# YOCO hybrid trunk on one core: deferred activations held in source order, an early GpSimd select, and two late evictions

## The chip, the cores and the metric

One core of one Trainium2 chip runs the kernel. The metric is device time in microseconds (us) of one execution, the median of several runs. The engines are TensorE (PE: matmuls), VectorE (DVE), ScalarE (ACT), GpSimd (POOL) and SyncE (SP, which issues most DMAs). Each engine works through its own queue in order; they wait for each other through semaphores.

## The reference, cut to what matters

Two layers on x of 1024 x 1024 float32. Layer one is a chunked gMLP, layer two attention in a sliding window of 128:

```
u, v, z = split(rms_norm(x) @ w_in, 3)      # each 1024 x 2048
u = gelu(u);  v = layer_norm(gelu(v))
s = einsum(causal(w_s), v per chunk of 128, 8 groups of 256 channels) + b_s
h = x + rms_norm((u * s * silu(z)) @ w_out)
k, v = rms_norm(h) @ w_k, @ w_v
q, z = split(rms_norm(h) @ w_in_b, 2)
o = softmax with sinks over a band of 128 (ALiBi), 16 query heads, 4 kv heads
out = h + rms_norm((o * silu(z)) @ w_out_b)
```

All matmuls are to be exact to nearly float32.

## The kernel before

**Matmuls.** Every operand is split into a high and a low part (`split`, L104: ScalarE copies the high part, L105; VectorE subtracts for the low part, L106; with a gain it is L109 and L110). A product is then three matmuls into one PSUM bank (`mm3`, L168: lines L169, L170, L171), each 128x512.

**Stage v** (`v_layer`, to about 145 us). v = x @ w_v is made in seven Strassen-Winograd products, in the order m = 1, 2, 5, 6, 7, 4, 3, for two halves Q = 0 and 1 of the columns, each m in two steps u = 0, 1. There are two sets of four PSUM banks, `vb` (m = 1, 6, 7, 4 accumulate in it) and `vc` (m = 2, 5, 3). At the ends of m = 1, 6 and 7 ScalarE copies the four tiles of `vb` out (L209); PE can add the next product to a bank of `vb` only after its copy. VectorE adds `vc` to the slots (L206). A finished block gets its gelu from `done` (L390 to L392): one ScalarE instruction per tile, `vslot<-vslot,rx` with the row scale `rx`, and one VectorE `bn_stats`. For two blocks of Q = 0 these are put off to a later step (`late`); for Q = 1 the first block's are called right at the end of m = 2. `rx` is 1/rms of x's rows: a small VectorE instruction (L178) and a power on GpSimd (L179). `broadcast_rstd` makes diagonals `dg` from it (ScalarE L279, VectorE L280) and spreads them with four matmuls (L284).

The inputs of each step come ahead of it: `prep(n + 2)` loads the next weight piece (SP), adds or subtracts pieces on VectorE (L206, `sch`, `vraw`) and splits them.

**Stage uz** (`uz_layer`, 150 to 480 us). 16 quads: for each of 8 groups g one of u and one of z, again seven products; `ub` is a PSUM bank that products 1, 6, 7 and 4 of a quad share, and ScalarE copies it out between them (L209). `normalise(g)` scales the eight pieces of the loaded v (VectorE L614), `spatial` makes the gating matmuls (L621), `finish` takes the silu of z (L630) and the u quads get four gelus (L697). Gelu and silu lie in different activation tables: ScalarE loads a table (ACT_TABLE_LOAD) at each change between them. The causal mask is a GpSimd affine_select on `wc` (L593), one per group.

**Stages out, q, kv, z.** `qz_four` (L958) makes four 128-column tiles of q or z. Its `evac` for q (L973 to L981) makes two ScalarE and two VectorE instructions per tile. `kv_phase` follows with the next weights, which `wnext` takes and splits one ahead.

**What sets the order.** The engines' orders are not those of the source. The framework's scheduler places each traced instruction on its engine's queue; an instruction that was traced later can stand ahead of one that waits for something late. `tc.keep_in_program_order(ins)` holds an instruction behind the one that was traced before it on its engine; it adds no wait.

Of the kernel before, what the change touches and what calls it, by code (L numbers as in the profile page):

```python
# [7 lines left out]
F32 = mybir.dt.float32  # L8
# [3 lines left out]
AF = mybir.ActivationFunctionType  # L12
ALU = mybir.AluOpType
# [9 lines left out]
G = 8  # L23
# [27 lines left out]
def tile_yoco(  # L51
# [111 lines left out]
    def wnext():  # L163
        w = weights.get()
        weights.ahead()
        return w
# [36 lines left out]
    HT = KT // 2  # L203

    def add(out, a, b, op, eng=None):
        (eng or nc.vector).tensor_tensor(out, a, b, op)  # L206

    def copy(out, a):
        nc.scalar.activation(out, a, AF.Copy)  # L209

    def xrow(h, t):
        return x[h * TH + t * P:h * TH + (t + 1) * P, :]
# [85 lines left out]
    def v_layer(ahead):  # L298
# [88 lines left out]
            dst = vd[2 * Q + i][4 * j:4 * j + 4]  # L387
            nc.scalar.dma_start(out=dst.rearrange("n p c -> p n c"), in_=block)

        def done(out, src, i, j, t, Q):  # L390
            nc.scalar.activation(out, src, AF.Gelu_apprx_tanh, scale=rx[j][:, t:t + 1])
            nc.vector.bn_stats(stats[:, 4 * j + t, 2 * Q + i], out)  # L392

        ORDER = (1, 2, 5, 6, 7, 4, 3)
# [24 lines left out]
        for k in range(2):  # L419
# [4 lines left out]
                                           ALU.mult, ALU.subtract)  # L424
            nc.vector.tensor_tensor(p0[1][:, cs], r0[:, cs], p0[0][:, cs].bitcast(F32), ALU.subtract)
        ready[0] = p0
        r1_ = load(raws.take("v1"), wv_in[0, 1])
        for k in range(2, 4):
            split_scaled(T[1][0][:, k], T[1][1][:, k], xa[:, 0, k], g(0, k))
# [10 lines left out]
        for n, (Q, m, u) in enumerate(steps):  # L440
# [24 lines left out]
            elif n >= 4:  # L465
                step(side)

            late = {(7, 0): (a1, 0), (3, 0): (e67, 1)}.get((m, u)) if Q == 0 else None
            if late:
                for t in range(4):  # L470
                    done(late[0][t], late[0][t], late[1], late[1], t, Q)
                store(slots[late[1]], late[1], late[1], Q)
            if u == 0:
                continue
            for t in range(4):
                if m == 1:
                    a1.append(slots[0][:, t])
                    copy(a1[t], ps[t])
                elif m == 2:
                    add(a1[t], a1[t], ps[t], ALU.add)  # L480
                    if Q:
                        done(a1[t], a1[t], 0, 0, t, Q)
                elif m == 6:
                    if t == 0:
                        e6 = big.tile([P, 4, TH], F32, tag="P1_3", name=f"ve6_{Q}")
                    copy(e6[:, t], ps[t])
                elif m == 7:
                    e67.append(slots[1][:, t])
                    copy(e67[t], ps[t])
                    add(e67[t], e67[t], bank_c[t], ALU.add)  # L490
                    if Q:
                        done(e67[t], e67[t], 1, 1, t, Q)
                elif m == 4:
                    c = slots[Q][:, t]
                    done(c, ps[t], 1, 0, t, Q)
                elif m == 3:
                    add(e6[:, t], e6[:, t], ps[t], ALU.add)
                    done(e6[:, t], e6[:, t], 0, 1, t, Q)
            block = {3: (e6, 0, 1), 4: (slots[Q], 1, 0)}.get(m)
            if Q and m in (2, 7):  # L500
                block = (slots[0], 0, 0) if m == 2 else (slots[1], 1, 1)
            if block:
                store(*block, Q)
            if m == 3:
# [10 lines left out]
    def uz_layer():  # L515
# [95 lines left out]
        def normalise(g):  # L611
            vg = grp[g]["vg"]
            for n in range(NB):
                nc.vector.tensor_scalar(vg[:, n], vg[:, n], mv[:, n, 0:1], ve[:, n:n + 1], ALU.subtract, ALU.mult)  # L614

        def spatial(g, i, j):
            d = grp[g]
# [9 lines left out]

        def finish(g, i, j):
            z = grp[g][1][i, j]
            nc.scalar.activation(z, z, AF.Silu)  # L630
            add(z, z, grp[g][0][i, j], ALU.mult)
            m = {(0, 0): 1, (1, 0): 2, (1, 1): 3}.get((i, j))
            if m:
                nc.sync.dma_start(out=td[m][g], in_=z)
# [30 lines left out]
        for q in range(len(quads) + 1):  # L665
# [20 lines left out]
            if q > 0:  # L686
                product(q - 1, 3, pcc, False)
                add(pc[0, 1], pc[0, 1], pcc, ALU.add)
                scale(pc[0, 1], 1)
                if pz:  # L690
                    finish(pg, 0, 1)
                    sums(pg)
                    del grp[pg]
                else:
                    for i in range(2):
                        for j in range(2):
                            nc.scalar.activation(pc[i, j], pc[i, j], AF.Gelu_apprx_tanh)  # L697
                del ops[q - 1]
            if not live:
                break  # L700
# [254 lines left out]
    half = [slice(0, 64), slice(64, P)]  # L955
    vt = big.tile([P, NB, 256], F32, tag="P1_1", name="vt")

    def qz_four(h, which, m, n, evac):  # L958

        tag = "s" if (h, which, m) in ((0, 0, 4), (0, 1, 0)) else "mm"  # L960
        ps = [bank(tag, f"qz{h}_{which}_{m + i}") for i in range(4)]
        for kq in range(4):
            hi, lo = (t.rearrange("p (m k c) -> p m k c", m=4, k=2) for t in wnext())
            for i in range(4):
                for kk in range(2):
                    k = 2 * kq + kk
                    mm3(ps[i], hi[:, i, kk], lo[:, i, kk], n[0][:, k], n[1][:, k], k == 0, k == KT - 1)
                if kq == 3:
                    evac(m + i, ps[i])
                yield  # L970

    def q_phase(h, n, q):
# [24 lines left out]
    def kv_phase(h, n):  # L997
        pk = [bank("mm", f"pk{h}_{i}") for i in range(2)]
        pv = [bank("mm", f"pv{h}_{i}") for i in range(2)]
        for kp in range(4):  # L1000
            hi, lo = wnext()
            for kk in range(2):
                k = 2 * kp + kk
                o = kk * 512
# [297 lines left out]
```

## Time and profile before

| | us |
|---|---|
| median of 3 runs | 1050.8 (1050.23 to 1050.91) |
| the profiled execution | 1051.19 |
| its span, first to last instruction | 1049.4 |
| PE busy in it | 1038.2 (99%) |
| DVE, ACT, POOL busy | 731.8, 579.8, 199.5 |
| granted TensorE clock, share of full speed | 0.998 |

The page is read in this order: the busy share of each engine, PE's list of waits, and then PE's timeline at each wait with the timelines of the engines named there. The span is shorter than the execution's own time by 1.8 us, which lies outside the first and last instruction.

### The profile page before, as it was taken

The numbers are of one execution on the slowest core, as the hardware profiler recorded it, in microseconds if no ns is written. First come the engines' busy times: TensorE is split into PE (matmuls) and PEld (weight loads), VectorE is DVE, ScalarE is ACT, GpSimd is POOL, SyncE is SP. The second block draws the span as 40 slices with busy tenths as digits, with TensorE's granted clock in tenths as the row PEclk, the third lists the DMA queues.
The fourth block names the chain that finished last, engine by engine and source line by source line (L and its number), as shares of the span: only waits on it lengthen the run. The fifth ranks groups of instructions, "written<-read, shape, count | busy, mean of one in ns | idle before, by whom it ended". The sixth has DMA issues, their size and how long they took to land.

```text
span 1049.4 us, 13678 instructions
## 1 busy us (share of the span) xinstructions
PE 1038.2 (99%) x4994; PEld 854.8 (81%) x4994; DVE 731.8 (70%) x1244; ACT 579.8 (55%) x998; POOL 199.5 (19%) x153
## 2 busy tenths in 40 slices
PE   9999999999999999999999999999999999999997
PEld 7878888888888888888888888888888777877776
DVE  6987566867768668677696587765247786667763
ACT  6584344565565465655444465654466665786631
POOL 0500003253442552530200000100001111011120
PEclk9999999999999999999999999999999999999999
DMA  8878242324333333247998543532322121211363
GB/s 309 271 262 292 101 171 94 116 101 146 126 117 120 123 134 116 101 140 265 320 354 282 195 167 93 200 102 82 99 81 66 56 81 61 81 61 62 121 220 121
DMA packets 80899, 157.56 MB, mean 150 GB/s; under 512 B 5824, under 2 KB 32704, under 8 KB 80832
## 3 DMA queue, kind: packets, MB, share of 16 engines
q1 hardware_dynamic: 76320, 148.01, 41.4%
q10 hardware_dynamic: 4512, 8.68, 2.3%
q8 instruction: 39, 0.64, 0.3%
q14 instruction: 28, 0.23, 0.1%
HBM read 125.21 MB, written 31.46 MB: 149 GB/s over the span
## 4 chain that ended last, share of the span: by engine, by line
PE 93%; DVE 3%; DMA 2%; ACT 1%; issue 0%; SPq 0%; DVEq 0%; POOLq 0%; ACTq 0%
PE qz L169 6%; PE ob L169 6%; PE ub L169 6%; PE qz L171 6%; PE ub L170 6%; PE ub L171 6%; PE ob L171 6%; PE ob L170 6%; PE qz L170 6%; PE s L1058 3%; PE uc L170 3%; PE uc L169 3%; PE uc L171 3%; PE sp L621 3%; PE oc L169 2%; PE oc L171 2%
## 5 line engine op out<-in xcount | busy, mean ns | idle before, releaser
L110 DVE SCALAR_TENSOR_TENSOR wlo<-raw_w,gn,whi 128x512 fp32r<-128x512 f32 x80 | 58.5, 757 | 62.2 <-ACT whi L109 62.0
L169 PE MATMUL qz<-n_hi,whi 128*128 128x512 f32 x256 | 100.9, 394 | 0.0
L171 PE MATMUL qz<-n_hi,wlo 128*128 128x512 f32 x256 | 99.8, 390 | 1.1 <-DVE wlo L110 1.1
L170 PE MATMUL qz<-n_lo,whi 128*128 128x512 f32 x256 | 99.9, 390 | 0.0
L109 ACT ACTIVATE whi<-raw_w,gn 128x512 fp32r<-128x512 f32 x80 | 54.8, 716 | 56.8 <-PE qz L170 36.6
L1073 ACT ACTIVATE pr<-pr,mx 128x129 f32<-128x129 f32 x128 | 50.1, 393 | 39.8 <-DVE mx L1069 39.8
L169 PEld LDWEIGHTS qz<-n_hi,whi 128*128 128x128 f32 x256 | 48.1, 188 | 15.8 <-issue 5.7
L105 ACT ACTIVATE uzhilo_g<-f 128x1024 fp32r<-128x1024 f32 x31 | 32.9, 1060 | 49.2 <-PE uc L171 43.3
L171 PEld LDWEIGHTS qz<-n_hi,wlo 128*128 128x128 f32 x256 | 48.0, 188 | 11.8 <-DVE wlo L110 1.5
L170 PEld LDWEIGHTS qz<-n_lo,whi 128*128 128x128 f32 x256 | 48.1, 188 | 9.3
L106 DVE TENSOR_TENSOR uzhilo_g<-f,uzhilo_g 128x1024 fp32r<-128x1024 f32 x31 | 38.6, 1245 | 19.9 <-ACT uzhilo_g L105 19.9
L209 ACT ACTIVATE uz_slots<-ub 128x512 f32<-128x512 f32 x48 | 28.3, 590 | 42.4 <-PE ub L171 39.2
L169 PE MATMUL ub<-T,whi_g 128*128 128x512 f32 x128 | 50.7, 396 | 0.0
L169 PE MATMUL ub<-T,uzhilo_g 128*128 128x512 f32 x128 | 50.5, 395 | 0.0
L171 PE MATMUL ub<-T,wlo_g 128*128 128x512 f32 x128 | 49.9, 390 | 0.0
L171 PE MATMUL ub<-T,uzhilo_g 128*128 128x512 f32 x128 | 49.9, 390 | 0.0
L170 PE MATMUL ub<-T,uzhilo_g 128*128 128x512 f32 x128 | 49.9, 390 | 0.0
L170 PE MATMUL ub<-T,whi_g 128*128 128x512 f32 x128 | 49.8, 389 | 0.0
L169 PE MATMUL uc<-T,uzhilo_g 128*128 128x512 f32 x124 | 48.9, 395 | 0.0
L170 PE MATMUL uc<-T,uzhilo_g 128*128 128x512 f32 x124 | 48.3, 389 | 0.0
L171 PE MATMUL uc<-T,uzhilo_g 128*128 128x512 f32 x124 | 48.3, 389 | 0.0
L105 ACT ACTIVATE whi_g<-raw_uz 128x1024 fp32r<-128x1024 f32 (+1 forms) x31 | 26.5, 854 | 36.8 <-PE ua L170 14.3
(334 smaller groups left out, 3078.3 us busy)
## 6 DMA issues: line engine op xcount, KB each, us to landing
raw_uz<-in_wuz_in_dram SPq DMA_DIRECT2D x32, 512.0 KB, 3.4
raw_w<-in_wqz_dram SPq DMA_DIRECT2D x32, 512.0 KB, 3.5
td<-uz_slots SPq DMA_DIRECT2D x56, 256.0 KB, 2.2
orawP2a<-td SPq DMA_DIRECT2D x28, 512.0 KB, 4.1
raw<-in_wv_in_dram SPq DMA_DIRECT2D x17, 512.0 KB, 4.8
vg<-vd SPq DMA_DIRECT2D x8, 1024.0 KB, 5.3
orawP2b<-in_wo_a_dram SPq DMA_DIRECT2D x16, 512.0 KB, 8.2
vraw<-in_wv_in_dram SPq DMA_DIRECT2D x13, 512.0 KB, 4.8
```

Source lines behind the costliest of these rows:

```text
L105: nc.scalar.activation(hi, src, AF.Copy)
L106: nc.vector.tensor_tensor(lo, src, hi.bitcast(F32), ALU.subtract)
L109: nc.scalar.activation(hi, src, AF.Copy, scale=g)
L110: nc.vector.scalar_tensor_tensor(lo, src, g, hi.bitcast(F32), ALU.mult, ALU.subtract)
L169: nc.tensor.matmul(out, lhsT=a_hi, rhs=b_hi, start=start, stop=False, skip_group_check=True)
L170: nc.tensor.matmul(out, lhsT=a_hi, rhs=b_lo, start=False, stop=False, skip_group_check=True)
L171: nc.tensor.matmul(out, lhsT=a_lo, rhs=b_hi, start=False, stop=stop, skip_group_check=True)
L209: nc.scalar.activation(out, a, AF.Copy)
L621: nc.tensor.matmul(psv[:, n], lhsT=d["vg"][:, 4 * j + n, i * P:(i + 1) * P], rhs=d["wc"], start=True, stop=True)
L1058: nc.tensor.matmul(pss[par][:, g, w0:256], lhsT=q[par][:, m, bs_], rhs=w[par][:, p, ks], start=g + k == 0, stop=g + k == 2, skip_group_che ...
L1073: nc.scalar.activation(pr[:, i], pr[:, i], AF.Exp, bias=mx[:, i:i + 1], scale=-1.0, accum_out=dn[:, i:i + 1])
```

## The change

Four edits.

1. In `v_layer`, the put-off gelus (`late`) are held in source order on ScalarE, and for Q = 1 the gelus of the first block move from the end of m = 2 to the step (5, 0), which makes them put-off ones too.
2. In `uz_layer`, the scalings of `normalise`, the silus of `finish` and the gelus of u are held in source order, silus and gelus except for the last group.
3. In `v_layer`, behind GpSimd's first two casts, GpSimd copies 128x2 numbers into `mv[:, 0]` (a tile that is written for good at the end of the stage) and runs a 128x2 affine_select on it.
4. In `qz_four`, for the second four tiles of the first q phase (h = 0, m = 4), the evictions of tiles 2 and 3 (qz_0_6, qz_0_7) are put off into `kv_phase`, behind its first `wnext()`.

```diff
+    pin = tc.keep_in_program_order
...
-        def done(out, src, i, j, t, Q):
-            nc.scalar.activation(out, src, AF.Gelu_apprx_tanh, scale=rx[j][:, t:t + 1])
+        def done(out, src, i, j, t, Q, put_off=False):
+            gelu = nc.scalar.activation(out, src, AF.Gelu_apprx_tanh, scale=rx[j][:, t:t + 1])
+            if put_off:
+                tc.keep_in_program_order(gelu)
             nc.vector.bn_stats(stats[:, 4 * j + t, 2 * Q + i], out)
...
         ready[0] = p0
+
+        nc.gpsimd.tensor_copy(mv[:, 0], p0[0][:, 1022:1024].bitcast(F32))
+        nc.gpsimd.affine_select(mv[:, 0], mv[:, 0], [[1, 2]], ALU.is_ge, 0.0, base=0, channel_multiplier=0)
...
-            late = {(7, 0): (a1, 0), (3, 0): (e67, 1)}.get((m, u)) if Q == 0 else None
+            late = ({(7, 0): (a1, 0), (3, 0): (e67, 1)}, {(5, 0): (a1, 0)})[Q].get((m, u))
             if late:
                 for t in range(4):
-                    done(late[0][t], late[0][t], late[1], late[1], t, Q)
+                    done(late[0][t], late[0][t], late[1], late[1], t, Q, True)
                 store(slots[late[1]], late[1], late[1], Q)
...
                     add(a1[t], a1[t], ps[t], ALU.add)
-                    if Q:
-                        done(a1[t], a1[t], 0, 0, t, Q)
...
-            if Q and m in (2, 7):
-                block = (slots[0], 0, 0) if m == 2 else (slots[1], 1, 1)
+            if Q and m == 7:
+                block = (slots[1], 1, 1)
...
-                nc.vector.tensor_scalar(vg[:, n], vg[:, n], mv[:, n, 0:1], ve[:, n:n + 1], ALU.subtract, ALU.mult)
+                pin(nc.vector.tensor_scalar(vg[:, n], vg[:, n], mv[:, n, 0:1], ve[:, n:n + 1], ALU.subtract, ALU.mult))
...
-            nc.scalar.activation(z, z, AF.Silu)
+            silu = nc.scalar.activation(z, z, AF.Silu)
+            if g + 1 < G:
+                pin(silu)
...
-                            nc.scalar.activation(pc[i, j], pc[i, j], AF.Gelu_apprx_tanh)
+                            gelu = nc.scalar.activation(pc[i, j], pc[i, j], AF.Gelu_apprx_tanh)
+                            if pg + 1 < G:
+                                pin(gelu)
...
                 if kq == 3:
-                    evac(m + i, ps[i])
+                    if (h, which, m) == (0, 0, 4) and i > 1:
+                        put_off.append((evac, m + i, ps[i]))
+                    else:
+                        evac(m + i, ps[i])
...
             hi, lo = wnext()
+            while put_off:
+                evac, m, ps = put_off.pop(0)
+                evac(m, ps)
```

How the order of instructions changes, at three places. Line numbers of the changed kernel are its own, 3 to 18 higher for the same code; the numbers behind a name count tiles.

**First place: stage v, Q = 0, the evictions of m = 6.** GpSimd's queue, from the first casts to the powers that make `rx` (`rx_87` for the first 512 rows, `rx_88` for the second), before:

```order
L422 CAST whi_v_140<-raw_v_133 128x512 x2
L593 ISA
L593 AFFINE_SELECT wc_1226<-wc_1226 128x128
L593 AFFINE_SELECT wc_1342<-wc_1342 128x128
L179 TENSOR_TENSOR rx_87<-rx_87,small 128x4
L179 TENSOR_TENSOR rx_88<-rx_88,small 128x4
```

and now:

```order
L427 CAST whi_v_140<-raw_v_133 128x512 x2
L433 COPY mv<-whi_v_140 128x2
L434 ISA
L434 AFFINE_SELECT mv<-mv 128x2
L599 AFFINE_SELECT wc_1228<-wc_1228 128x128
L599 AFFINE_SELECT wc_1344<-wc_1344 128x128
L179 TENSOR_TENSOR rx_87<-rx_87,small 128x4
```

A copy and a 128x2 select stand right behind the casts, and the ISA instruction, which the first affine_select brings with it, moves there. ScalarE's queue at the four copies of `vb` out to `ve`, before:

```order
L209 ACTIVATE ve_0_497<-vb_0_174 128x512
L209 ACTIVATE ve_0_497<-vb_1_175 128x512
L209 ACTIVATE ve_0_497<-vb_2_176 128x512
L391 ACTIVATE vslot_126<-vslot_126,rx_87 128x512
L209 ACTIVATE ve_0_497<-vb_3_177 128x512
L105 ACTIVATE whi_533<-vraw_12_531 128x1024
L105 ACTIVATE T_526<-tch 128x1024
L183 ACTIVATE junk_x_0_540,ssx_537<-vraw_xs_0_538 128x1024
L391 ACTIVATE vslot_126<-vslot_126,rx_87 128x512 x3
```

and now:

```order
L212 ACTIVATE ve_0_499<-vb_0_176 128x512
L212 ACTIVATE ve_0_499<-vb_1_177 128x512
L212 ACTIVATE ve_0_499<-vb_2_178 128x512
L282 ACTIVATE dg_921<-ident,rx_87 128x128
L212 ACTIVATE ve_0_499<-vb_3_179 128x512
L105 ACTIVATE whi_535<-vraw_12_533 128x1024
L105 ACTIVATE T_528<-tch 128x1024
L183 ACTIVATE junk_x_0_542,ssx_539<-vraw_xs_0_540 128x1024
L394 ACTIVATE vslot_126<-vslot_126,rx_87 128x512 x4
```

The gelu `vslot_126<-vslot_126,rx_87` between the third and the fourth copy has gone behind the next splits, to the other three. In its place stands a small instruction of `broadcast_rstd`, the diagonal `dg<-ident,rx_87`, which needs `rx_87` too.

**Second place: stage v, Q = 1, the end of m = 2.** VectorE's queue where the first block gets the `vc` banks added, before:

```order
L106 TENSOR_TENSOR wlo_910<-sch_870,whi_909 128x1024
L206 TENSOR_TENSOR sch_870<-sch_870,raw_01_1013 128x1024
L206 TENSOR_TENSOR vslot_126<-vslot_126,vc_0_842 128x512
L206 TENSOR_TENSOR vslot_126<-vslot_126,vc_1_843 128x512
L206 TENSOR_TENSOR vraw_13_1075<-vraw_13_1075,sch_870 128x1024
L392 BN_STATS bst<-vslot_126 128x6 x2
L206 TENSOR_TENSOR vslot_126<-vslot_126,vc_2_844 128x512
L206 TENSOR_TENSOR vslot_126<-vslot_126,vc_3_845 128x512
L106 TENSOR_TENSOR vlo_986<-sch_870,vhi_985 128x1024
```

and now:

```order
L106 TENSOR_TENSOR wlo_912<-sch_872,whi_911 128x1024
L206 TENSOR_TENSOR sch_872<-sch_872,raw_01_1015 128x1024
L206 TENSOR_TENSOR vslot_126<-vslot_126,vc_0_844 128x512
L206 TENSOR_TENSOR vslot_126<-vslot_126,vc_1_845 128x512
L206 TENSOR_TENSOR vraw_13_1077<-vraw_13_1077,sch_872 128x1024
L206 TENSOR_TENSOR vslot_126<-vslot_126,vc_2_846 128x512
L206 TENSOR_TENSOR vslot_126<-vslot_126,vc_3_847 128x512
L106 TENSOR_TENSOR vlo_979<-sch_872,vhi_978 128x1024
L397 BN_STATS bst<-vslot_126 128x6 x4
```

The two `bn_stats` between the second and the third addition have gone behind the split `vlo`. On ScalarE the two gelus that stood ahead of the high part of that split (`vhi`) have gone behind it as well. On PE the new order has one matmul instead of three of the next product (`vb_0` alone) ahead of the first matmul of m = 5, `vc_0<-whi`.

**Third place: stage uz, an example of ScalarE's queue around the gelus of a u quad** (`uz_slots` and `uz_slots4` are the slots that hold the products, `ub7` the PSUM bank of quad 7), before:

```order
L209 ACTIVATE uz_slots4_1333<-ub7_2395 128x512
L105 ACTIVATE whi_g1_8_2437<-raw_uz8_0_2376 128x1024
L697 ACTIVATE uz_slots4_1333<-uz_slots4_1333 128x512
L105 ACTIVATE whi_g4_7_2462<-raw_uz7_1_2206 128x512
L630 ACT_TABLE_LOAD
L630 ACTIVATE uz_slots4_1333<-uz_slots4_1333 128x512
L105 ACTIVATE uzhilo1_g3_7_2459<-f2_7_2368 128x1024
L697 ACT_TABLE_LOAD
L697 ACTIVATE uz_slots_1332<-uz_slots_1332 128x512
L209 ACTIVATE uz_slots4_1333<-ub7_2395 128x512
```

and now:

```order
L212 ACTIVATE uz_slots4_1335<-ub7_2397 128x512
L105 ACTIVATE whi_g1_8_2439<-raw_uz8_0_2378 128x1024
L705 ACT_TABLE_LOAD
L705 ACTIVATE uz_slots_1334<-uz_slots_1334 128x512
L105 ACTIVATE whi_g4_7_2464<-raw_uz7_1_2208 128x512
L105 ACTIVATE uzhilo1_g3_7_2461<-f2_7_2370 128x1024
L705 ACTIVATE uz_slots_1334<-uz_slots_1334 128x512
L705 ACTIVATE uz_slots4_1335<-uz_slots4_1335 128x512 x2
L212 ACTIVATE uz_slots4_1335<-ub7_2397 128x512
```

The four gelus of quad 6 stand together behind one table load, three of them ahead of the second copy of `ub7`; before, a silu with a table load of its own stood between them. At these two lines 17 table loads stand in the whole stage where there were 43.

## Rows read from the trace of the kernel before

**Rows 1.** Busy time of each engine by stretch of the run (start:end of the stretch in us, its length, then each engine's busy us with its instructions, the granted clock, the DMA share and GB/s).

```profile
50.00:75.00 25.00, 23.71 (x105) 19.30 (x104) 21.87 (x32) 20.66 (x35) 4.09 (x4) 1.00 0.77 262
...
100.00:125.00 25.00, 24.70 (x109) 20.09 (x109) 15.48 (x17) 7.95 (x11) 0.00 (x0) 1.00 0.47 170
...
150.00:480.00 330.00, 330.00 (x1576) 277.15 (x1575) 236.47 (x352) 179.87 (x218) 128.95 (x95) 1.00 0.37 126
...
675.00:700.00 25.00, 23.95 (x106) 19.44 (x105) 15.95 (x23) 13.78 (x21) 1.80 (x1) 1.00 0.33 106
```

**Rows 2.** Timeline of TensorE around 52 to 58 us (start, duration, engine, line, operation, output<-inputs, shape; in brackets the idle time before it and what ended it).

```profile
52.65 0.39 PE L171 MATMUL vb<-vhi,T 128*128 128x512 f32 x1
54.33 0.50 PE L169 MATMUL vb<-vhi,T 128*128 128x512 f32 x1 [1.29 <-ACT ve L209]
...
57.88 0.39 PE L169 MATMUL vb<-whi,T 128*128 128x512 f32 x1
```

**Rows 3.** Timeline of ScalarE in the same stretch (the columns as in Rows 2).

```profile
53.07 0.72 ACT L391 ACTIVATE vslot<-vslot,rx 128x512 f32<-128x512 f32 x1 [2.11 <-POOL rx L179]
53.70 0.58 ACT L209 ACTIVATE ve<-vb 128x512 f32<-128x512 f32 x1
```

**Rows 4.** The select line L593 by itself: all its instructions on GpSimd (count, shortest/median/longest in ns, first and last start).

```profile
L593 POOL TENSOR_SCALAR_AFFINE_SELECT wc<-wc x8: 294/297/11536, 39.0 to 412.4; 128x128 f32<-128x128 f32 x8
```

**Rows 5.** Timeline of GpSimd, 38 to 53 us (x2: two instructions in one row).

```profile
39.02 13.03 POOL L593 TENSOR_SCALAR_AFFINE_SELECT wc<-wc 128x128 f32<-128x128 f32 x2 [30.87 <-DMA wc<-in_ws_t_dram]
52.03 1.01 POOL L179 TENSOR_TENSOR rx<-rx,small 128x4 f32<-128x4 f32 x1
```

**Rows 6.** Timeline of VectorE, 49 to 51 us.

```profile
49.18 1.21 DVE L106 TENSOR_TENSOR wlo<-raw,whi 128x1024 fp32r<-128x1024 f32 x1
50.32 0.27 DVE L178 TENSOR_SCALAR rx<-ssx 128x4 f32<-128x4 f32 x1
```

**Rows 7.** Line L279 by itself, ScalarE's half of the diagonal (columns as in Rows 4).

```profile
L279 ACT ACTIVATE dg<-ident,rx x8: 385/388/391, 69.1 to 94.7; 128x128 fp32r<-128x128 f32 x8
```

**Rows 8.** Timeline of TensorE, 104 to 109 us.

```profile
104.12 0.39 PE L169 MATMUL vc<-vhi,T 128*128 128x512 f32 x1
...
106.62 0.39 PE L171 MATMUL vc<-vhi,T 128*128 128x512 f32 x1
106.84 1.07 PE L284 MATMUL bc<-dg,ones_r 128*128 128x512 f32 x4
108.22 0.97 PE L169 MATMUL vb<-vhi,T 128*128 128x512 f32 x3 [0.30 <-ACT vhi L105]
109.02 0.40 PE L169 MATMUL vc<-whi,T 128*128 128x512 f32 x1
```

**Rows 9.** Timeline of ScalarE, 101 to 108 us.

```profile
101.60 1.06 ACT L105 ACTIVATE whi<-sch 128x1024 fp32r<-128x1024 f32 x1 [3.59 <-PE vc L171]
105.82 1.34 ACT L391 ACTIVATE vslot<-vslot,rx 128x512 f32<-128x512 f32 x2 [3.15 <-DVE vslot L206]
107.10 1.06 ACT L105 ACTIVATE vhi<-sch 128x1024 fp32r<-128x1024 f32 x1
```

**Rows 10.** Timeline of VectorE, 99 to 110 us.

```profile
99.96 1.23 DVE L206 TENSOR_TENSOR sch<-sch,raw 128x1024 f32<-128x1024 f32 x1 [0.69 <-DMA raw<-in_wv_in_dram]
...
102.70 1.23 DVE L106 TENSOR_TENSOR wlo<-sch,whi 128x1024 fp32r<-128x1024 f32 x1 [0.25 <-ACT whi L105]
...
105.10 1.28 DVE L206 TENSOR_TENSOR vslot<-vslot,vc 128x512 f32<-128x512 f32 x2
106.30 1.22 DVE L206 TENSOR_TENSOR vraw<-vraw,sch 128x1024 f32<-128x1024 f32 x1
107.43 1.28 DVE L392 BATCH_NORM_STATS2 bst<-vslot 128x6 f32<-128x512 f32 x2
108.63 1.27 DVE L206 TENSOR_TENSOR vslot<-vslot,vc 128x512 f32<-128x512 f32 x2
```

**Rows 11.** Timeline of VectorE around the q matmuls.

```profile
681.87 0.76 DVE L980 SCALAR_TENSOR_TENSOR q_lo<-qz,qsc,q_lo 64x512 fp32r<-64x512 f32 x1
682.66 2.74 DVE L110 SCALAR_TENSOR_TENSOR wlo<-raw_w,gn,whi 128x512 fp32r<-128x512 f32 x4
...
704.00 0.75 DVE L110 SCALAR_TENSOR_TENSOR wlo<-raw_w,gn,whi 128x512 fp32r<-128x512 f32 x1
```

**Rows 12.** Timeline of TensorE at the two places that take those weights.

```profile
683.46 0.50 PE L171 MATMUL qz<-n_hi,wlo 128*128 128x512 f32 x1 [1.05 <-DVE wlo L110]
...
706.77 0.47 PE L169 MATMUL pk<-n_hi,whi 128*128 128x512 f32 x1
```

**Rows 13.** ScalarE's costliest groups in 150 to 480 us (line, engine, operation, count, then busy us and mean ns of one, then idle before).

```profile
L630 ACT ACT_TABLE_LOAD x21 | 26.9, 1283 | 0.4
L697 ACT ACT_TABLE_LOAD x21 | 26.9, 1283 | 0.4
```

**Rows 14.** ScalarE in 312 to 324 us, timeline.

```profile
316.83 0.58 ACT L209 ACTIVATE uz_slots<-ub 128x512 f32<-128x512 f32 x1
```

**Rows 15.** TensorE in 320 to 324 us, timeline.

```profile
322.58 0.48 PE L169 MATMUL ub<-T,uzhilo_g 128*128 128x512 f32 x1
```

**Rows 16.** List of waits in 150 to 480 us (engine and line, what it waited for: us in total, times, longest us).

```profile
ACT uz_slots L697 <- DVE uz_slots L206: 14.8, 16, 3.7
```

**Rows 17.** Timeline of VectorE near the start of the run.

```profile
8.19 0.69 DVE L425 TENSOR_TENSOR wlo_v<-raw_v,whi_v 128x512 fp32r<-128x512 f32 x1 [0.98 <-POOL whi_v L422]
```

More of the change, by code (lines that the diff above doesn't have):

```diff
@@ L205, in add @@
     def add(out, a, b, op, eng=None):
-        (eng or nc.vector).tensor_tensor(out, a, b, op)
+        return (eng or nc.vector).tensor_tensor(out, a, b, op)
+    pin = tc.keep_in_program_order
     def copy(out, a):
-        nc.scalar.activation(out, a, AF.Copy)
+        return nc.scalar.activation(out, a, AF.Copy)
     def xrow(h, t):
@@ L956, in tile_yoco @@
     vt = big.tile([P, NB, 256], F32, tag="P1_1", name="vt")
+    put_off = []
     def qz_four(h, which, m, n, evac):
```

## The prediction

> **What bounds the kernel now.** I read the busy time by stretches first. In most of them TensorE is busy for the whole stretch: in all of stage uz, 150 to 480 us, its 330.00 us are full. The changed code touches three stretches with holes: 50 to 75 us (23.71 of 25), 100 to 125 us (24.70) and 675 to 700 us (23.95) [rows 1]. So PE bounds the kernel, and an edit can gain only what it takes out of these holes, which the page shows as three waits: 1.29 us for the copy `ve`, 0.30 us for the split `vhi`, 1.05 us for the weights' `wlo` [rows 2, 8, 12].
>
> How long one 128x512 matmul takes in the stream: from 104.12 to 106.62 eleven start one after another, 2.50 / 11 = 0.227 us each [rows 8]. The true cost of the first wait is read with it: 52.65 to 57.88 holds 16 matmuls, 16 x 0.227 = 3.64, and took 5.23 [rows 2]; so 1.59 us, more than the 1.29 in brackets, since the matmuls behind a hole start slower.
>
> The cause of that wait is a chain across four engines. PE waits for the fourth copy of `vb`. ScalarE made it at 53.70, because the gelu ahead of it in its queue sat 2.11 us for `rx` [rows 3]. GpSimd made `rx` at 52.03 to 53.04, though its input from VectorE was there at 50.32 + 0.27 = 50.59 [rows 5, 6]: ahead of it stood two affine_selects from 39.02 to 52.05. The first of the eight selects took 11.54 us, the median is 0.297 [rows 4, 5]. So the first one pays some 11.2 us once, which I take for code that is loaded at the first use, and the pair leaves 1.49 for the second.
>
> **The change part by part.**
>
> *The early select.* It moves the first use to right behind the casts, about 8.2 us. GpSimd had nothing to do for the 30.87 us before 39.02 [rows 5], so 11.5 us end near 20 and hide there, at no cost. The two real selects then take some 0.3 us each, and GpSimd is free when `rx`'s input comes at 50.59. The power takes 1.01 [rows 5], so `rx` is there at about 51.6.
>
> *The held gelus, first place.* The gelu of 0.72 us leaves the place between the third and fourth copy, but the diagonal that stands there now needs `rx` as well. It takes 0.39 [rows 7]: 51.60 + 0.39 + 0.58 for the copy = 52.57. PE wants the fourth bank at 52.65 + 0.23 = 52.88 [rows 2]. It fits by 0.3 us, and the wait goes: **-1.59 us**. The ends: if the second select keeps its 1.49 us and its end at 52.05, `rx` comes at 53.04 as before and only the shorter instruction gains, 0.72 - 0.39 = 0.33. So -0.33 to -1.59. I take -1.59, as the two edits together clear the chain; without the early select the diagonal would wait just as the gelu did.
>
> *The held gelus, second place.* Before, ScalarE's split `vhi` at 107.10 stood behind two gelus [rows 9]. Taking them out alone gains next to nothing: PE still reads the buffer that `vhi` overwrites until its last matmul of m = 2, started at 106.62, ends at about 107.0 [rows 8]. Now PE would come 1.59 us sooner, and what is late next decides. That is VectorE's chain: `sch` at 99.96 is released by a weight's DMA [rows 10], and the DMA's time hangs on the queue before it, not on PE. From there a split, three additions of whole pieces and the additions of the banks follow without a gap to 108.63. PE's first matmul of m = 5 needs a bank of `vc`, by the new order one that the third addition frees. Before, that addition ran from 108.63 to about 109.27 (1.28 for two) [rows 10]. Two terms bring it forward. The two `bn_stats` ahead of it are gone: 108.63 - 107.43 = 1.20. The split at 102.70 waited for ScalarE's, which began only at 101.60, held up by PE [rows 9, 10]; with PE earlier it starts when VectorE's addition ends, 99.96 + 1.23 = 101.19, and VectorE goes on without its gap of 0.25 and a little sooner, about 0.35 in all. So the bank is free at 109.27 - 1.20 - 0.35 = 107.72. Before, PE began m = 5 at 109.02 with three matmuls of the next product already made, now with one: the like moment before is 109.02 - 2 x 0.227 = 108.57 [rows 8]. What is left of the gain behind this place is 108.57 - 107.72 = 0.85 us; the other **+0.74 us** are given back. The ends: if the DMA comes as much earlier as PE does, nothing is given back; if VectorE gets no 0.35 and `bn_stats` from earlier places stand in its way (0.6 each), all but 0.2 is. I take the middle, as the row at 99.96 names the DMA.
>
> *Stage uz.* 43 table loads become 17. They cost ScalarE 1.283 us each [rows 13], so 33 us less work on ScalarE, but PE has no wait there and the gain is **0**. Could it lose? Three gelus now stand ahead of the second copy of a `ub` bank. That copy ran at 316.83, PE takes the bank at 322.58 [rows 14, 15]: 5.17 us of cover, against 3 x 0.63 = 1.9 us of gelus. The scalings of `normalise` move back on VectorE behind work that PE waits for sooner. I take 0; what it costs if the cover is gone is the rival below.
>
> *q's late evictions.* The third wait is at 683.46, for a `wlo` that VectorE began at 682.66, right behind the evictions of q's first four tiles (the last at 681.87) [rows 11, 12]. The change puts off tiles 6 and 7, of the second four, some 17 us later, where the next weights' `wlo` ends at 704.75 and PE takes it at 706.77 [rows 11, 12]. 2 us of cover there are no gain, and the order ahead of 682.66 is the same. **0**; the ends are 0 and -1.3 (1.05 and the slower start behind it).
>
> The sum: -1.59 + 0.74 = -0.85. The profiled execution of 1051.19 would be about 1050.35. It lies 0.4 above the median of the runs shown, 1050.8, so the **median becomes about 1050.0**.
>
> *A rule against the early select.* VectorE's subtraction of two inputs in SBUF at 8.19 [rows 17] and those after it would now run beside the loading select. While the long select ran before, such a subtraction at 49.18 took 1.21 us [rows 6], and I saw 1.22 to 1.23 for it with GpSimd idle (102.70 [rows 10]). The Trainium skill, "SBUF — State Buffer", section "Who interferes with whom", says that a VectorE instruction with two SBUF inputs contends with a GpSimd instruction that reads SBUF, and that the one which comes second is blocked for the whole of the other. By that rule the start could lose up to the select's length; the row at 49.18 speaks against it, and I keep it as a rival with a small chance.
>
> **The rivals.**
>
> *A. Nothing is given back at 107 us.* The DMA comes earlier with PE, or the bank is freed by an earlier addition. For it: VectorE had gaps before, so its chain may move. Against: the row at 99.96. Then -1.6: 1049.2.
>
> *B. The change doesn't do what it says at the first wait.* `rx` is late in spite of the early select, because the second select's 1.49 us were its own, or the long first time goes with the tile and not with the first use. For it: the cover is 0.3 us. Against: the median of eight selects is 0.297. Then between 0 and -0.3: about 1050.6.
>
> *C. The third wait goes as well,* by VectorE coming to 682.66 earlier. For it: less work on ScalarE ahead. Against: no order changes there. Then -0.85 - 1.3 = -2.15 to -2.9: 1048.3.
>
> *D. Slower: the held gelus make the copy of `ub` late.* ScalarE's longest wait for an operand of these gelus was 3.7 us [rows 16]. Held in order, such a wait now holds the copy: 3.7 + 1.9 = 5.6, against 5.17 of cover, so 0.43 us late, in seven u quads 3.0 us. It decides from the point where the first gelu waits over 3.3 us. Against: the long waits came up where the gelu stood far ahead of its operand. Then 1050.0 + 3.0 = 1053.0.
>
> *E. Slower: GpSimd's long select blocks VectorE at the start.* The subtraction at 8.19 would start at up to 19.8, and PE with it: up to 11 us, 1061. It decides from the first VectorE subtraction that runs while the select does; against it stands the row at 49.18.
>
> **How the numbers follow.** Forecast 0.57, A 0.18, B 0.12, C 0.06, D 0.05, E 0.02. About 0.2% (2.1 us) is what a measurement of this kernel can tell from no change; the forecast, A and B all lie within it. So faster 0.06, same 0.87, slower 0.07. The range goes from A with a little more (1048.8) to B with the spread of the runs (1051.2); it leaves out C, D and E.
>
> **What the profile of the changed kernel would show.** The first select of about 11.5 us near 8 us, and those near 39 and 50 us at 0.3; no wait of PE near 53 us, its matmuls at 57 us about 1.6 us earlier; near 106 to 108 us a wait of about a microsecond, now for VectorE's addition; the wait near 682 us as large as before; no wait in stage uz and some 33 us less of ScalarE's busy time. I would be wrong if PE waits anywhere in 150 to 480 us, if VectorE's subtractions around 8 to 20 us take over 1.3 us, or if the wait at 682 us is gone.

## The result, and the profile after

| | before | changed |
|---|---|---|
| median of 20 runs, us | 1050.62 (1049.55 to 1051.48) | 1052.92 (1049.49 to 1053.59) |
| profiled execution, its span | 1051.19, 1049.4 | 1053.16, 1051.5 |
| PE, DVE, ACT busy | 1038.2, 731.8, 579.8 | 1039.5, 750.9, 546.4 |

The ratio of changed to before is 1.0018, with a 95% interval of 1.0011 to 1.0024: slower by some 2 us, within the 0.2% called no change, but above the stated range. The changed kernel's 20 runs fall into two groups: twelve from 1052.58 to 1053.59, where the mean granted clock was 0.996 or 0.997, and eight from 1049.49 to 1051.70 at 0.998 or 0.999.

By stretches, the changed kernel (columns as in [rows 1]):

```profile
50.00:75.00 25.00, 22.71 (x93) 18.33 (x93) 21.38 (x31) 19.90 (x33) 5.01 (x4) 0.93 0.72 242
...
100.00:125.00 25.00, 24.71 (x109) 20.15 (x108) 16.82 (x18) 8.05 (x11) 0.00 (x0) 1.00 0.46 166
...
150.00:480.00 330.00, 330.00 (x1576) 277.36 (x1575) 254.77 (x351) 146.01 (x192) 131.32 (x95) 1.00 0.37 125
...
675.00:700.00 25.00, 24.33 (x108) 19.75 (x107) 15.20 (x22) 13.80 (x22) 2.57 (x2) 1.00 0.33 109
```
The first row has it all: PE has 22.71 us of 25 where it had 23.71, and the granted clock of the stretch is 0.93 where it was 1.00. Stage uz is as full as before, and the stretch from 675 us is better by 0.4. PE's list of waits says the same:

```profile
PE vb L169 <- ACT ve L212: 2.3, 1, 2.3
...
PE qz L171 <- DVE wlo L110: 0.7, 1, 0.7
```
I set the start of each PE instruction against that of the like one before. It comes 0.1 us later up to 47 us, 2.7 later at 72 us, the same up to 163 us, 0.2 less from 175 us on, and 0.4 less again behind 683 us: +2.6, -0.2, -0.4. So the whole loss lies between 47 and 72 us. GpSimd's timeline there, which answers to [rows 5], and its select line, which answers to [rows 4]:

```profile
9.12 0.19 POOL L434 TENSOR_SCALAR_AFFINE_SELECT mv<-mv 128x2 f32<-128x2 f32 x1
39.42 14.06 POOL L599 TENSOR_SCALAR_AFFINE_SELECT wc<-wc 128x128 f32<-128x128 f32 x2 [30.11 <-DMA wc<-in_ws_t_dram]
53.46 1.01 POOL L179 TENSOR_TENSOR rx<-rx,small 128x4 f32<-128x4 f32 x1
```
```profile
L599 POOL TENSOR_SCALAR_AFFINE_SELECT wc<-wc x8: 497/665/11247, 39.4 to 415.2; 128x128 f32<-128x128 f32 x8
```
The early 128x2 select was the first of the execution, and it took 0.19 us. The next, at 39.42, took 11.25 as if there had been no earlier one; the second select then took 2.8 where it had taken 1.49. So the long time does not come with the first affine_select of an execution; a first one of full size is tried in e3. VectorE's timeline shows what stands beside it:

```profile
48.15 1.22 DVE L106 TENSOR_TENSOR T<-xa,T 128x1024 fp32r<-128x1024 f32 x1
49.29 1.22 DVE L106 TENSOR_TENSOR wlo<-raw,whi 128x1024 fp32r<-128x1024 f32 x1
50.42 0.27 DVE L178 TENSOR_SCALAR rx<-ssx 128x4 f32<-128x4 f32 x1
50.60 2.73 DVE L359 SCALAR_TENSOR_TENSOR tch<-xb,gn,tch 128x512 f32<-128x512 f32 x4
```
The first long select ends at 39.42 + 11.25 = 50.67, which is 0.25 behind the start of L178 at 50.42. The one of before ended at 39.02 + 11.54 = 50.56, 0.24 behind its L178 at 50.32 [rows 4 to 6]. L178 is the first instruction in a long stream that reads one SBUF input; all those ahead of it from 39 us on read two and follow each other without a gap. The second select ends at 53.49, 0.16 behind the end of the next such stream (50.60 + 2.73 = 53.33). That stream has four instructions now and had two before, since `bn_stats`, which waits for the gelus, went behind the other two.

ScalarE and PE behind that (ScalarE first; the columns as in [rows 2, 3]):

```profile
54.51 0.40 ACT L282 ACTIVATE dg<-ident,rx 128x128 fp32r<-128x128 f32 x1 [3.44 <-POOL rx L179]
54.81 0.58 ACT L212 ACTIVATE ve<-vb 128x512 f32<-128x512 f32 x1
```
```profile
55.44 0.79 PE L169 MATMUL vb<-vhi,T 128*128 128x512 f32 x1 [2.29 <-ACT ve L212]
56.03 0.63 PE L170 MATMUL vb<-vlo,T 128*128 128x512 f32 x1
...
58.95 0.40 PE L171 MATMUL vb<-vhi,T 128*128 128x512 f32 x1
...
60.57 0.39 PE L169 MATMUL vb<-whi,T 128*128 128x512 f32 x1
```
`rx` came at 54.47, 1.43 later than before, and the diagonal `dg` waited for it in the place where the gelu had, in front of the fourth copy. PE's hole grew from 1.29 to 2.29. And behind it seven matmuls from 56.03 to 58.95 took 2.92 us, 0.42 each in place of 0.227. PE's clock, two microseconds at a time (the number behind the engines is the granted clock):

```profile
54.00:56.00 2.00, 0.56 (x1) 0.50 (x2) 0.00 (x0) 1.49 (x3) 0.47 (x1) 0.86 0.02 6
56.00:58.00 2.00, 2.00 (x6) 1.57 (x5) 1.63 (x2) 2.00 (x3) 0.00 (x0) 0.50 0.00 0
58.00:60.00 2.00, 2.00 (x8) 1.59 (x8) 1.76 (x3) 2.00 (x5) 0.00 (x0) 0.79 0.59 207
60.00:62.00 2.00, 2.00 (x11) 1.63 (x10) 2.00 (x4) 2.00 (x4) 0.00 (x0) 1.00 0.91 366
```
It is 0.50 of full speed from 56 to 58 us, the lower of the two levels (1.2 of 2.4 GHz), and full again from 60 us.

### The profile page after: what moved, and what is told of

Read it like the earlier page. It is cut to its first block, busy times and chain, and to the rows that moved or that the text cites. A ratio compares the mean times of both kernels' runs of the same rounds, so it can differ in the third digit from the quotient of the medians.

```text
span 1051.5 us, 13665 instructions
## 1 busy us (share of the span) xinstructions
PE 1039.5 (99%) x4994; PEld 855.7 (81%) x4994; DVE 750.9 (71%) x1244; ACT 546.4 (52%) x972; POOL 203.8 (19%) x155
## 4 chain that ended last, share of the span: by engine, by line
PE 97%; DMA 1%; DVE 0%; ACT 0%; SPq 0%; issue 0%; DVEq 0%; POOLq 0%; ACTq 0%
PE qz L169 6%; PE ob L169 6%; PE ub L169 6%; PE qz L171 6%; PE ub L171 6%; PE ub L170 6%; PE ob L171 6%; PE ob L170 6%; PE qz L170 6%; PE s L1076 3%; PE uc L170 3%; PE uc L169 3%; PE uc L171 3%; PE sp L627 3%; PE vb L170 3%; PE vb L171 3%
## 5 line engine op out<-in xcount | busy, mean ns | idle before, releaser
L171 PEld LDWEIGHTS qz<-n_hi,wlo 128*128 128x128 f32 x256 | 48.1, 188 | 11.5 <-DVE wlo L110 1.1
L620 DVE TENSOR_SCALAR vg<-vg,mv,ve 128x256 f32<-128x256 f32 x64 | 47.5, 795 | 0.0
L206 POOL TENSOR_TENSOR f<-raw_uz,raw_uz 128x512 f32<-128x512 f32 x15 | 21.6, 1442 | 124.9 <-DVE uzhilo_g L106 124.9
```

Source lines behind the costliest of these rows:

```text
L171: nc.tensor.matmul(out, lhsT=a_lo, rhs=b_hi, start=False, stop=stop, skip_group_check=True)
L206: return (eng or nc.vector).tensor_tensor(out, a, b, op)
L620: pin(nc.vector.tensor_scalar(vg[:, n], vg[:, n], mv[:, n, 0:1], ve[:, n:n + 1], ALU.subtract, ALU.mult))
```

## Experiments

Theory P: a GpSimd instruction that reads SBUF waits as long as VectorE runs instructions with two SBUF inputs without a gap, and is let in at the first one that has one input, or at a gap. Theory L, that of the prediction: the first use of the select pays once. e1, e2, e3, e8, e9, e10 and e12 are single runs; e4 to e7 are medians of eleven runs and e11 of ten, and in brackets stands the ratio to the kernel before, run beside them, with its 95% interval.

**e1 and e2: a small door in VectorE's stream.** The kernel before, and in e1 behind another subtraction of m = 7 than in e2:

```diff
+    tick = const.tile([P, 4], F32, name="tick")
...
+    tc.keep_in_program_order(nc.vector.tensor_scalar(tick, nhalf, 1.0, 0.0, ALU.mult, ALU.add))
```

> The kernel before with one more small VectorE instruction (a 128x4 multiply-add with one SBUF input, the same kind as L178) between two two-input subtractions, at about 40.2 us. Theory P (GpSimd's select waits as long as VectorE runs two-input instructions back to back, and gets in at the first one with one input): the first select starts at about 39.0 and ends within 0.4 us of the small instruction, so it lasts about 1.5 us in place of 11.5. Theory L (a cost paid once at the first use of the select): it lasts 11.2 to 11.5 us wherever the small instruction stands.

> The same small instruction, one place of the stream later, at about 44.7 us. Theory P: the first select ends within 0.4 us of it and lasts about 5.9 us. Theory L: 11.2 to 11.5 us as before.

VectorE and GpSimd of e1, then of e2:

```profile
41.55 1.22 DVE L107 TENSOR_TENSOR wlo<-sch,whi 128x1024 fp32r<-128x1024 f32 x1
42.69 0.27 DVE L355 TENSOR_SCALAR tick<-small 128x4 f32<-128x4 f32 x1
```
```profile
39.46 3.48 POOL L596 TENSOR_SCALAR_AFFINE_SELECT wc<-wc 128x128 f32<-128x128 f32 x1 [31.12 <-DMA wc<-in_ws_t_dram]
```
```profile
44.88 0.27 DVE L380 TENSOR_SCALAR tick<-small 128x4 f32<-128x4 f32 x1
```
```profile
39.64 5.49 POOL L596 TENSOR_SCALAR_AFFINE_SELECT wc<-wc 128x128 f32<-128x128 f32 x1 [31.93 <-DMA wc<-in_ws_t_dram]
```
The small instruction stood at 42.69 in e1, not at 40.2 as I had expected, since VectorE does that step later; in e2 at 44.88. The select ended at 42.94 and at 45.13, both times some 0.25 behind it. A cost of the first use would not move with the small instruction, so L fails here.

Is it the one input that lets the select in, or only that the instruction is small? The six later selects of `wc`, in stage uz, tell. In the kernel before they run among the scalings of `normalise` (`vg`, 128x256, one tensor input and two columns of scalars), which follow each other without a gap, and five of the six take 0.29 to 0.30 us, one 0.47. In the changed kernel each starts within a two-input addition of 0.69 us, takes 0.50 to 0.72 and ends 0.15 to 0.16 behind that addition. The first of the six, VectorE and GpSimd, before:

```profile
202.60 2.35 DVE L614 TENSOR_SCALAR vg<-vg,mv,ve 128x256 f32<-128x256 f32 x7 [0.70 <-DMA vg<-vd]
202.89 0.30 POOL L593 TENSOR_SCALAR_AFFINE_SELECT wc<-wc 128x128 f32<-128x128 f32 x1 [2.12 <-DMA wc<-in_ws_t_dram]
```
and in the changed kernel:

```profile
205.03 0.69 DVE L206 TENSOR_TENSOR uz_slots<-uz_slots,uz_slots 128x512 f32<-128x512 f32 x1 [0.70 <-ACT uz_slots L636]
205.28 0.60 POOL L599 TENSOR_SCALAR_AFFINE_SELECT wc<-wc 128x128 f32<-128x128 f32 x1 [2.08 <-DMA wc<-in_ws_t_dram]
```
So larger one-input instructions leave the select alone too, as P has it. The times of e1 and e2, 1068.79 and 1068.65, are another matter (e9).

**e3: a first select of full size.** The kernel before, with a 128x128 select on a scratch area.

```diff
+        nc.gpsimd.memset(bc[:, 0, 0:P], 1.0)
+        nc.gpsimd.affine_select(bc[:, 0, 0:P], bc[:, 0, 0:P], [[1, P]], ALU.is_ge, 0.0, base=0, channel_multiplier=-1)
```

> The kernel before with a select of the full size (128x128, same pattern) on a scratch area right behind GpSimd's first casts, in place of the 128x2 one of the change. Theory P: the select near 39 us still ends right behind L178 (near 50.6), 11.2 to 11.5 us, since what stands on VectorE is the same. Theory L in its second form (the cost is paid once by the first select of full size, the 128x2 one was too small to pay it): the early one takes some 11 us, the one near 39 us about 0.3 to 0.7.

GpSimd, its select line, and VectorE of e3:

```profile
1.07 0.29 POOL L428 TENSOR_SCALAR_AFFINE_SELECT bc<-bc 128x128 f32<-128x128 f32 x1
...
46.94 4.13 POOL L595 TENSOR_SCALAR_AFFINE_SELECT wc<-wc 128x128 f32<-128x128 f32 x2 [38.68 <-DMA wc<-in_ws_t_dram]
```
```profile
L595 POOL TENSOR_SCALAR_AFFINE_SELECT wc<-wc x8: 287/292/3877, 46.9 to 415.6; 128x128 f32<-128x128 f32 x8
```
```profile
50.57 0.27 DVE L178 TENSOR_SCALAR rx<-ssx 128x4 f32<-128x4 f32 x1
```
The first select took 0.29 us at 1.07, where VectorE did nothing. The one of `wc` came late (its data landed at 46.9) and still lasted 3.88 us, to 50.82: again 0.25 behind L178. L falls in its second form too. The run took 1053.96, because the scheduler also put VectorE's first splits in another order: PE waited 4.2 us at the start, and behind that wait its granted clock was 0.50 from 12 to 14 us.

**e4 and e5: the diagonals held as well, with and without the early select.** In e4 the changed kernel's `broadcast_rstd` is cut in two; the diagonals are made at the end of Q = 0 and held. e5 is e4 without the two early GpSimd instructions.

```diff
+    def make_diags(pool):
+        pin(copy(ones_r, ones))
...
+                pin(nc.scalar.activation(dg[:, 0, j], ident, AF.Copy, scale=r))
...
+                if (Q, m) == (0, 3):
+                    make_diags(vp)
```

> The changed kernel with the diagonals dg made at the end of Q = 0 and held there in source order on ScalarE, so that the four copies of vb to ve stand together. Theory P: rx is still late (54 us), but nothing that waits for it stands ahead of the fourth copy, so the 2.29 us hole of PE near 53 us and the lower clock behind it go; PE is there 4.1 to 4.2 us ahead of the changed kernel. By the prediction's second place 0.7 us are given back near 107 us: 1049.5; if nothing is given back 1048.8. Rival: the four gelus that now wait for rx hold up ScalarE's next splits, and PE waits a few us later instead: 1050.6 or more.

> The kernel of e4_diag_held without the early copy and select. Theory P: the early select does nothing, so the same time within 0.4 us and a first select of about 11 us near 39 us in both. Theory L: without it rx comes later than with it, and whatever waits for rx is later.

e4: 1049.57 (ratio to before 0.9988, 0.9979 to 0.9997); e5: 1049.65 (0.9988, 0.9979 to 0.9997). GpSimd of e5:

```profile
39.16 13.64 POOL L606 TENSOR_SCALAR_AFFINE_SELECT wc<-wc 128x128 f32<-128x128 f32 x2 [31.20 <-DMA wc<-in_ws_t_dram]
```
The selects took as long as ever and `rx` came at 54.8, but PE had no hole: in both it did 25.00 us of work in 50 to 75 us. So it was the diagonal in front of the fourth copy that made `rx` matter, and the early select does nothing. In e5's profile PE was 1.6 us ahead of before behind the place and stayed so at 118 us. In e4's it lost 1.2 of them on the way, at the wait for a split below; that execution, 1051.21, is the slowest of e4's eleven.

```profile
96.17 0.50 PE L170 MATMUL vc<-wlo,T 128*128 128x512 f32 x1 [0.94 <-DVE wlo L106]
```
**e6: the rest alone.** The kernel before with edits 2 and 4 only.

> The kernel before with the uz stage's held gelus, silus and scalings and q's late evictions alone (nothing changed in stage v). If the whole loss is the first place in stage v: 0 to 0.6 us faster than before, 1050.0 to 1050.6, with PE's hole of 1.3 us near 53 us unchanged. Rival (the held order costs in stage uz): over 1051.

1050.79 (0.9997, 0.9988 to 1.0005): no difference that can be measured. PE's hole near 53 us is there as before:

```profile
PE vb L169 <- ACT ve L212: 1.3, 1, 1.3
```
**e7: q's first evictions put off too.** e4, and

```diff
-                    if (h, which, m) == (0, 0, 4) and i > 1:
+                    if (h, which, m) in ((0, 0, 0), (0, 0, 4)) and i > 1:
```

with the put-off ones done behind `wnext()` in `qz_four`.

> The kernel of e4_diag_held with tiles 2 and 3 of q's first four put off behind the next weights' split too, so that VectorE makes wlo ahead of the last evictions. If the hole near 682 us comes from those evictions: it goes, 0.9 to 1.3 us faster than e4_diag_held. Rival (the hole is bound by the weight buffers' release): the same as e4_diag_held.

1049.00 (0.9983, 0.9974 to 0.9992), 0.6 below e4, though the intervals of the two overlap, and less than the 0.9 to 1.3 expected: in e4's profile the hole was only 0.5. The interval is clear of 1, so e7 is faster than the kernel before, by some 1.9 us. Both holes are gone from its profile, and the wait for `wlo` from its list:

```profile
50.00:75.00 25.00, 25.00 (x113) 20.68 (x111) 23.36 (x32) 22.85 (x35) 2.96 (x3) 1.00 0.84 296
...
675.00:700.00 25.00, 25.00 (x121) 21.02 (x120) 16.61 (x24) 14.01 (x21) 1.15 (x1) 1.00 0.32 104
```
Its select shows one thing more (GpSimd, then VectorE):

```profile
39.62 7.90 POOL L608 TENSOR_SCALAR_AFFINE_SELECT wc<-wc 128x128 f32<-128x128 f32 x1 [30.43 <-DMA wc<-in_ws_t_dram]
```
```profile
46.15 1.22 DVE L206 TENSOR_TENSOR raw<-raw,sch 128x1024 f32<-128x1024 f32 x1
47.32 1.28 DVE L106 TENSOR_TENSOR vlo<-vraw,vhi 128x1024 fp32r<-128x1024 f32 x1
```
It ended at 39.62 + 7.90 = 47.52, 0.20 behind the start of `vlo`, with no one-input instruction near. `vlo` started 1.17 us behind the instruction ahead of it, where the others of this stream start 1.14 apart. In e9 (below), the kernel before with another layout, the first select ended early at the same place, at 39.46 + 7.86 = 47.32 (GpSimd, then VectorE):

```profile
39.46 7.86 POOL L595 TENSOR_SCALAR_AFFINE_SELECT wc<-wc 128x128 f32<-128x128 f32 x1 [31.28 <-DMA wc<-in_ws_t_dram]
```
```profile
45.95 1.22 DVE L208 TENSOR_TENSOR raw<-raw,sch 128x1024 f32<-128x1024 f32 x1
47.08 1.31 DVE L108 TENSOR_TENSOR vlo<-vraw,vhi 128x1024 fp32r<-128x1024 f32 x1
```
There `vlo` did not start late (1.13 behind), but it lasted 1.31 in place of 1.22. What the two runs share is that `vlo` began 0.03 and 0.07 us behind the end of ScalarE's `vhi`, which it reads; in the runs where the select stayed out past `vlo`, 0.10 us or more lay between. So a two-input instruction that has only just got its operand may let the select in too. That was not tried, and P as worded does not cover e9.

**e8: the changed kernel again.** No edit.

> The changed kernel once more, for a second look at what differs between its executions (1049.5 to 1053.6). Theory P: the two selects of wc end 0.2 to 0.3 us behind the first VectorE instruction with one input or the first gap in VectorE's stream, wherever that falls in this execution; where PE's hole is about 2.3 us the granted clock is lower for some us behind it and the run is near 1053, where it is shorter the clock stays and the run is near 1051.5 or less. Rival: the clock drops in both, and the two groups of times have another cause.

1051.33, with this PE timeline and this stretch:

```profile
55.42 0.50 PE L169 MATMUL vb<-vhi,T 128*128 128x512 f32 x1 [2.28 <-ACT ve L212]
55.76 0.39 PE L170 MATMUL vb<-vlo,T 128*128 128x512 f32 x1
```
```profile
50.00:75.00 25.00, 22.72 (x100) 18.48 (x100) 21.66 (x32) 20.23 (x34) 5.28 (x4) 1.00 0.72 251
```
The hole is the same (2.28), the second select's end too (53.47), but the clock stayed at 1.00 and the matmuls went on at full pace. PE lost 1.0 us against before in place of 2.6. So the 1.6 us between these two executions are the lower clock, and the mean clocks of the 20 runs divide their two groups the same way. My guess that a shorter hole keeps the clock up is wrong: the same hole does both, and what decides stays open. The kernel before is not quite free of it: one of its 13 runs beside e8 took 1053.41 at a mean granted clock of 0.997.

**e9, e10, e12: why e1 and e2 took 1068.** The kernel before with an unused tile of 16, 64 or 128 bytes per partition among the constants.

```diff
+    pad = const.tile([P, 4], F32, name="pad")
+    nc.vector.memset(pad, 0.0)
```

> The kernel before with one unused 16-byte tile per partition among the constants, which the allocator rounds to 32 bytes, so that the large tiles start at 32 bytes past a multiple of 64; no instruction is added but a memset at the start. If the start of the tiles is what made e1 and e2 17 us slower: about 1068, with every 128x512 matmul some 3.5 ns longer. Rival (the small VectorE instruction or the other order made them slower): 1050 to 1051.

> The same with a tile of 64 bytes, so that the large tiles start at multiples of 64 again. If the start of the tiles counts: 1050 to 1051.5. Rival (any other layout costs): as e9.

> The kernel before with an unused 128-byte tile among the constants, so that the weights' tiles start at a multiple of 128 bytes again, as in the kernel before; with 64 bytes they started at 64 past one (e10), with 32 at 32 past one (e9). If the start of these tiles relative to 128 bytes is what lengthens the matmuls: 1050 to 1051.5. Rival (any shift of the layout costs): 1060 or more.

1068.73, 1064.61 and 1066.49. One group of PE's matmuls (count, busy us, mean ns) in the kernel before, in e9 and in e12:

```profile
L170 PE MATMUL qz<-n_lo,whi 128*128 128x512 f32 x256 | 99.9, 390 | 0.0
```
```profile
L172 PE MATMUL qz<-n_lo,whi 128*128 128x512 f32 x256 | 101.3, 396 | 0.0
```
```profile
L172 PE MATMUL qz<-n_lo,whi 128*128 128x512 f32 x256 | 101.0, 394 | 0.0
```
In most groups a 128x512 matmul is 4 to 6 ns longer, from the first stage to the last; a few, such as `ob<-wob_hi,q_hi` (392 before, 393 in e9), are not. In e9 no wait is added. So neither the small instruction nor the order made e1 and e2 slow, but the shifted places of tiles. My rules for it failed: not the start relative to 64 bytes (e10), nor to 128 (e12). What in the layout counts stays open.

**e11: the changed kernel with a door.** The small instruction, into a cell that exists.

```diff
+                if (Q, u) == (0, 0):
+                    pin(nc.vector.tensor_scalar(small[:, 4:5], small[:, 0:1], 1.0, 0.0, ALU.mult, ALU.add))
```

> The changed kernel with one small one-input VectorE instruction (128x1, into a cell that exists, so no tile moves) in the stream near 45 us. Theory P: the first select ends within 0.4 us of it, the second right behind L178 near 50.5, so rx no longer waits for selects; the order of ScalarE also changes (a sum of squares stands where dg stood). No hole of 2.3 us near 53 us, no lower clock: 1049 to 1050.2. Theory L: a first select of 11 us and 1052.9 as the changed kernel, if the order on ScalarE gives nothing.

1050.16 (0.9991, 0.9981 to 1.0000), 1.0 below the kernel before on that chip (1051.2). VectorE, GpSimd and PE:

```profile
44.84 0.14 DVE L382 TENSOR_SCALAR small<-small 128x1 f32<-128x1 f32 x1
```
```profile
39.48 5.60 POOL L601 TENSOR_SCALAR_AFFINE_SELECT wc<-wc 128x128 f32<-128x128 f32 x1 [30.19 <-DMA wc<-in_ws_t_dram]
50.40 0.32 POOL L601 TENSOR_SCALAR_AFFINE_SELECT wc<-wc 128x128 f32<-128x128 f32 x1 [5.32 <-DMA wc<-in_ws_t_dram]
```
```profile
53.77 0.50 PE L169 MATMUL vb<-vhi,T 128*128 128x512 f32 x1 [0.39 <-ACT ve L212]
```
The first select ended at 45.08, 0.24 behind the door, the second in 0.32, and `rx` came at 52.67 in place of 54.47. PE's hole is 0.39. The order on ScalarE changed as well (no `dg` between the copies), so the two parts are not told apart by the time; the select's end is the point here.

## Why the prediction was wrong

**The step that failed** is "the first one pays some 11.2 us once, which I take for code that is loaded at the first use". The runs show a wait in its place: VectorE's stream keeps the select out for those 11.2 us (e1, e2, e11), and a first select that meets no such stream takes 0.29 (e3). The rows were there: the long select's end stood 0.24 us behind the start of L178 [rows 4 to 6]. I read where it began and not what happened where it ended.

**The rule I weighed held, the other way round.** I weighed only whether GpSimd would block VectorE, and found the subtraction at 49.18 unhurt. The Trainium skill, "SBUF — State Buffer", section "Who interferes with whom", also says that issue order decides who blocks. This trace agrees: VectorE, which was there first and left no gap, lost nothing (1.21 to 1.22 us each), and a select of 0.3 us lasted 11.5, over ten VectorE instructions in a row. Rival E did not come up: the early select took 0.19 us.

**The first place**, -1.59, came out as +2.6. With `rx` no earlier, the diagonal stood where the gelu had been. My rival B saw that `rx` might stay late, and gave it -0.33 for the shorter instruction. It missed that the moved `bn_stats` lengthen VectorE's stream from two instructions to four, which keeps the second select out 1.4 us longer: +1.0 for PE (e8), and in most runs 1.6 more by the lower clock, for which the prediction has no term. The size of the stall itself was right: with the diagonal out of the way PE gains 1.6 there (e4, e5, e7).

**The second place**, +0.74, could not come up in the changed kernel, where PE came late. Where PE came early, e5 gave nothing back. VectorE's rows of e5 that answer to [rows 10]:

```profile
97.47 1.23 DVE L206 TENSOR_TENSOR sch<-sch,raw 128x1024 f32<-128x1024 f32 x1
...
105.90 1.28 DVE L206 TENSOR_TENSOR vslot<-vslot,vc 128x512 f32<-128x512 f32 x2
```
The addition that I took for held by the DMA (99.96) stood 2.5 us earlier, and the one I took for the next bound ran at 105.90. So the chain moved with PE, as rival A had it. e4's profile did give back 1.2, but at 96 us and for another split; what made it late there was not tried. The time of e5, 1049.65, would also fit 0.7 given back, but its trace has that loss elsewhere: PE's last matmul starts 2.2 us earlier than before (1040.03, before 1042.26), and the span ends only 1.4 earlier (1048.0, before 1049.4). So 0.8 us went behind the last matmul; why was not tried.

**Stage uz at 0**: near enough. PE is 0.2 us better there in every kernel with the held order; rival D did not come up. e6, with edits 2 and 4 alone, shows no difference that can be measured.

**q's late evictions at 0**: right in that they do not touch the hole at 682 us by their order. It shrank from 1.05 to 0.67, to 0.5 in e8, the same kernel, to 0.8 in e6, where nothing in stage v is changed, and to 0.8 in e3, where nothing in q is. So it differs from run to run with q's order as it was; why was not settled. That the hole comes from the evictions of q's first four tiles is shown by e7.

**The time**: 1052.92 against 1050.0. Of the 2.6 us that PE lost, the hole made 1.0 and the clock 1.6; 0.6 came back later.

## What to carry to other kernels

When an instruction lasts forty times its usual time, look at what another engine does at the moment it ends, before calling it a first-use cost. A GpSimd instruction on the path should not sit beside a gapless stream of two-input VectorE work: one small one-input instruction there opens it, and taking its reader off the path is safer still (e4, e5). Holding one instruction in source order moves others into its place: read in the new order what stands there, and whether it waits for the same thing.

## What the runs showed that I had not expected

- GpSimd's first long select ended 0.24 to 0.25 us behind the start of a one-input VectorE instruction in twelve of the fourteen profiled executions, wherever that instruction stood. In e7 and e9 it ended 0.20 and 0.24 behind the start of a two-input one.
- After the same hole of 2.3 us PE's granted clock fell to 0.50 for some 3 us in one execution and stayed at 1.00 in another; 1.6 us lie between them.
- 16 to 128 more bytes among the constants lengthened most matmuls by 4 to 6 ns of 390 and the kernel by 13 to 18 us, in single runs.
